# Values stationary, normed probabilities moving in the attention, and other positions of the mixer's stages

## The chip, the core and the metric

The kernel runs on one core of a Trainium2 chip. The metric is the device time of one execution in microseconds. Before the change it is 1552.36 us, the median of three runs (1552.14 to 1554.68).

A core has engines that work side by side, each through its own queue in order: TensorE (PE; its weight loads are PEld), VectorE (DVE), ScalarE (ACT), GpSimd (POOL) and SyncE (SP), which issues nearly all DMAs here. [...] An instruction at the head of a queue that waits holds up everything behind it.

## What is computed

One layer of a decoder: half a SwiGLU step, a mixer with two branches, half a SwiGLU step, norms around them. 512 real positions and 16 meta tokens, width 1024. The change lies in the attention branch of the mixer: 16 query heads of 64, two key/value groups, a window of 128 positions, meta tokens always visible, and a sink per head.

```python
q, kq, vq, rw, gates = jnp.split(u @ w_in[l], cols, axis=-1)
att = sliding_window_attention(rope(q), rope(kq), vq, sinks[l])
rwo = rwkv7_time_mix(*lerped(rw), ...)        # the other branch, a recurrence over time
merged = (jax.nn.sigmoid(g_att) * (att @ w_attn_branch[l])
          + jax.nn.sigmoid(g_rwkv) * (rwo @ w_rwkv_branch[l]))
h = h + merged @ w_out[l]

def sliding_window_attention(q, k, v, sinks):  # per block of queries, per head
    m = jnp.maximum(jnp.max(s, axis=-1, keepdims=True), sink)
    e = jnp.exp(s - m)
    p = e / (jnp.sum(e, axis=-1, keepdims=True) + jnp.exp(sink - m))
    o = jnp.einsum('bnhgqs,bnshd->bnqhgd', p, vals)
```

(The calls are shortened here.) All of it is float32.

## The kernel before

Three stages follow each other: FFN 1 (to about 425 us of the span), the mixer (to about 1130) and FFN 2. The dense products everywhere are made of three passes, L155 to L157: each weight is split into a high part `whi` (L144, ScalarE) and a low part `wlo` (L145, VectorE), each activation into `uh` and `ul`.

The mixer is written as generators: `qkv`, then for each of eight pairs of heads j the stages `stage_a1`, `stage_p`, `stage_i`, `stage_b`, `stage_t` of the recurrent branch, and beside them `att` (the function `attend`, in eight parts), `gate`, `att_branch`, `reload` and `rwkv_branch`. `run` steps through them: always the generator whose next step has the lowest position. `PLAN` gives each an offset and a span in units of one j, `STEPS` the number of steps that share the span, `SHIFT` a correction for one stage of one j, `ATTS` and `GATE` the distance between parts, and `LATE` moves the priority of what a stage issues. The tile scheduler then orders each engine's queue by priority and by what it takes to be ready. So a change of a table moves instructions on all queues.

What the steps of the prediction touch:

- `attend` works on blocks of 64 queries (b = 0 to 7), each in two passes i. A pass handles four of the eight query heads of each key/value group. L567, twice a pass: scores, 128 rows (2 heads x 64 queries) by two groups by n keys, n = 80, 144, then 208. L569: mask and maximum on VectorE. L582: four exponentials on ScalarE, which also give the sums. L584, L585: sink added, reciprocal `rsum`. L591: transposes of the unnormed probabilities, at most 128 keys at a time (one or two parts), L593: copy to `pT`. L600: the value product. L603: normalisation. L608: two transposes. L611: copy. L613: two stores to `aD` in HBM. All PSUM tiles of `attend` come from one bank (`att`), so each must be read before the next is written.
- `stage_b` is the recurrence of pair j over nine chunks: L928 (TensorE), L929 copy of z (ScalarE), L936 (TensorE), L937 and L938 copies into W (VectorE, ScalarE), L941 (TensorE), L947 (L945 in the first chunk) the next W (VectorE). Each step needs the one before.
- `stage_i` inverts triangular blocks on VectorE: L865 loads `LT` from HBM, then L870 and L872 alternate 31 times. `LT` has one buffer, which the end of the stage before (L898, L908) still reads.
- `att_branch` reads `aD` in eight pieces and multiplies by the branch weights `wa`, whose rows `prepare` has put in the order in which `aD` holds the heads.

Of the kernel before, what the change touches and what calls it, by code (L numbers as in the profile page):

```python
# [8 lines left out]
F32 = mybir.dt.float32  # L9
# [4 lines left out]
OP = mybir.AluOpType  # L14
# [3 lines left out]
P = 128  # L18
D = 1024
# [9 lines left out]
CH = 64  # L29
# [7 lines left out]
RB = {"g1": 2, "g2": 2, "W": 2, "g3": 2}  # L37
COUNTS = []
PAUSE = {"sq": 1, "rn": 1, "el": 1, "inv": 1}
PLAN = {"qkv": (-2.771, 0.729), "stage_a1": (-2.83, 0.789), "stage_p": (-1.171, 0.942), "stage_i": (-2.734, 0.587),  # L40
        "stage_b": (-0.138, 0.693), "stage_t": (1.478, 0.214), "att": (-1.614, 1.044), "gate": (0.091, 0.42),
        "att_branch": (3.86, 1.399), "reload": (6.425, 0.417), "rwkv_branch": (7.903, 0.124)}
STEPS = {"qkv": 30, "stage_a1": 19, "stage_p": 13, "stage_i": 9, "stage_b": 27, "stage_t": 5, "att": 13, "gate": 2, "att_branch": 24, "reload": 7,
         "rwkv_branch": 16}

SHIFT = {("stage_t", 5): -0.415, ("stage_i", 7): 0.482, ("stage_b", 2): 0.071, ("stage_a1", 6): -0.027, ("stage_i", 4): -0.133,
        ("stage_t", 2): -0.095, ("stage_b", 3): 0.119, ("stage_p", 1): 0.042, ("stage_t", 4): 0.123, ("stage_t", 3): -0.157,
        ("stage_t", 0): 0.003, ("stage_i", 6): 0.096, ("stage_p", 2): 0.173, ("stage_i", 3): -0.27, ("stage_i", 2): -0.033,
        ("stage_a1", 3): 0.319, ("stage_p", 6): 0.183, ("stage_a1", 4): 0.07, ("stage_p", 3): -0.095, ("stage_i", 1): 0.055,
# [2 lines left out]
        ("stage_t", 7): -0.124, ("stage_t", 1): -0.07, ("stage_i", 0): 0.174, ("stage_p", 5): -0.03, ("stage_b", 7): -0.047}  # L52

FIRST = [(0, 0), (0, 1), (1, 0), (1, 1), (27, 0)]
ATTS = 0.946
GATE = 0.462
LATE = {"gate": 337, "att_branch": 1714, "reload": 1055, "rwkv_branch": 2849, "stage_a1": -79, "stage_t": 196, "stage_p": -207,
        "stage_i": -1108, "qkv": -36, "att": 209, "stage_b": 148}
S_DECAY = float(np.exp(np.float32(-0.5)))
GN_EPS = 64e-5  # L60
RMS_EPS = 1e-6
# [47 lines left out]
def hybrid_layer(ctx: ExitStack, tc: tile.TileContext, a, phases="all"):  # L109
    nc = tc.nc  # L110
    g = Ctx()
# [9 lines left out]
    bank = lambda: sm.tile([P, 512], F32, name="pn")  # L121
# [219 lines left out]
    aD = a["aD"] if "aD" in a else dram.tile([P, KD, SEQ], F32, name="aD")  # L341
# [4 lines left out]
    ident = C("ident")  # L346

    LO, HI = slice(0, 64), slice(64, 128)
# [4 lines left out]
    def mixer(nm):  # L353
# [7 lines left out]
        ap = es.enter_context(tc.tile_pool(name="mx_a", bufs=2))  # L361
# [3 lines left out]
        def bank(tag):  # L365
            if tag in SMALL:
                return small[:, SMALL[tag]]
            return ps.tile([P, 512], F32, name="p" + tag, tag=tag, bufs=BANKS[tag])
# [168 lines left out]
        def attend():  # L537
# [3 lines left out]
            for b in range(NCH):  # L541
# [18 lines left out]
                for i in range(2):  # L560

                    st = ap.tile([P, 2, 2, 208], F32, name="st", bufs=1)
                    mx = ap.tile([P, 2, 2], F32, name="mx")
                    for k in range(2):
                        pt = bank("att")[:, :416].rearrange("p (g s) -> p g s", g=2)
                        hp = 2 * i + k
                        nc.tensor.matmul(pt[:, :, :n], qb[:, P * hp:P * hp + P], kx[:, :, :n], start=True, stop=True)  # L567
                        for kv in range(2):
                            nc.vector.tensor_tensor_reduce(out=st[:, kv, k, :n], in0=pt[:, kv, :n], in1=am, scale=0.125,  # L569
                                                           scalar=NEG, op0=OP.add, op1=OP.max, accum_out=mx[:, kv, k:k + 1])  # L570
                        yield
                    sink = vec[:, VEC["sink"]:VEC["sink"] + 8].rearrange("p (g i k) -> p i g k", g=2, i=2)[:, i]
                    nm = ap.tile([P, 2, 2], F32, name="nm")
                    sm = ap.tile([P, 2, 2], F32, name="sm")
                    rsum = ap.tile([P, 2, 2], F32, name="rsum")
                    nc.vector.tensor_max(out=mx, in0=mx, in1=sink)
                    nc.vector.tensor_scalar(out=nm, in0=mx, scalar1=-1.0, scalar2=None, op0=OP.mult)
                    nc.vector.tensor_sub(out=sm, in0=sink, in1=mx)
                    nc.scalar.activation(out=sm, in_=sm, func=AF.Exp)
                    for x in range(4):  # L580
                        kv, k = x // 2, x % 2
                        nc.scalar.activation(out=st[:, kv, k, :n], in_=st[:, kv, k, :n], func=AF.Exp, bias=nm[:, kv, k:k + 1],  # L582
                                             accum_out=rsum[:, kv, k:k + 1])
                    nc.vector.tensor_add(out=rsum, in0=rsum, in1=sm)  # L584
                    nc.vector.reciprocal(out=rsum, in_=rsum)  # L585
                    yield
                    pTs = []
                    for q, (k0, k1) in enumerate(parts):
                        pt = bank("att")
                        for x in range(4):  # L590
                            nc.tensor.transpose(out=pt[:k1 - k0, P * x:P * x + P], in_=st[:, x // 2, x % 2, k0:k1], identity=ident)  # L591
                        pT = ap.tile([P, 512], F32, name="pT")
                        nc.scalar.copy(out=pT[:k1 - k0], in_=pt[:k1 - k0])  # L593
                        pTs.append(pT)
                    yield
                    po = bank("att")[:, :4 * CH].rearrange("t (p d) -> t p d", p=4)
                    for x in range(4):
                        kv = x // 2
                        for q, (k0, k1) in enumerate(parts):
                            nc.tensor.matmul(po[:, x, :], pTs[q][:k1 - k0, P * x:P * x + P], vt[:k1 - k0, q, CH * kv:CH * kv + CH],  # L600
                                             start=(q == 0), stop=(q == len(parts) - 1))
                    on = ap.tile([P, 4, CH], F32, name="ao", bufs=1)
                    nc.vector.tensor_tensor(out=on, in0=po, in1=rsum.rearrange("p g k -> p (g k)").unsqueeze(2).to_broadcast([P, 4, CH]),  # L603
                                            op=OP.mult)
                    yield
                    pt = bank("att")
                    for kv in range(2):
                        nc.tensor.transpose(out=pt[:, P * kv:P * kv + P], in_=on[:, 2 * kv:2 * kv + 2, :].rearrange("t p d -> t (p d)"),  # L608
                                            identity=ident)
                    ao = ap.tile([P, 2, 2, CH], F32, name="ao", bufs=1)  # L610
                    nc.scalar.copy(out=ao, in_=pt[:, :4 * CH].rearrange("p (g x t) -> p g x t", g=2, t=CH))  # L611
                    for kv in range(2):
                        nc.sync.dma_start(out=aD[:, 4 * kv + 2 * i:4 * kv + 2 * i + 2, CH * b:CH * b + CH], in_=ao[:, kv])  # L613
                    yield

        def gates():
# [444 lines left out]
        for j in range(NJ):  # L1061
            if j:
                ts.append(g[0])
            g = ()
# [110 lines left out]
def prepare(x, meta_tokens, norm_ffn1, ffn1_w_in, ffn1_w_out, norm_mix, w_in, rwkv_mu, sinks, w0, w2, a0, a2, g2, k_k, k_a,  # L1175
# [29 lines left out]
    b = np.concatenate([g2[0][P:]] * 3 + [np.zeros((32, D), np.float32)], 0)  # L1205
    d["g2s"] = np.ascontiguousarray(np.stack([g2[0][:P], b], 1).reshape(P, 2, KD, P).transpose(2, 0, 1, 3))

    wa = w_attn_branch.reshape(1, 4, 2, 2, CH, D).transpose(0, 1, 3, 2, 4, 5).reshape(1, D, D)
    for n, w in (("wa", wa), ("wr", w_rwkv_branch), ("wo", w_out)):
        d[n] = pack_w(w[0])  # L1210
    return d
# [17 lines left out]
```

## Time and profile before

| what | value |
|---|---|
| median of three runs | 1552.36 us |
| the profiled execution's own time | 1557.82 us |
| its span, first to last instruction | 1556.1 us |
| mean granted clock of TensorE | 0.980 |
| instructions | 25641 |
| HBM read, written | 140.03 MB, 21.52 MB |

The profile is one execution, 5.4 us over the median; a sum made from its rows is made against 1557.82. In a row of a group stand the source line, the engine and operation, the tile written and the tiles read (their numbers left out), the size, the count, then times. "PE patt L600: 8.5, 6" under such rows means: 8.5 us of idle time, in 6 places, ended when that instruction was done. In the timeline the last bracket is the idle time of the engine before the row and what ended it; "x16" joins 16 like instructions that follow each other. A matmul's own duration overlaps with its neighbours', so the distance from one start to the next is what counts. f32 matmuls appear in the trace as two passes, transposes as one.

### The profile page before, as it was taken

The numbers are of one execution on the slowest core, as the hardware profiler recorded it, in microseconds if no ns is written. First come the engines' busy times: TensorE is split into PE (matmuls) and PEld (weight loads), VectorE is DVE, ScalarE is ACT, GpSimd is POOL, SyncE is SP. The second block draws the span as 40 slices with busy tenths as digits, with TensorE's granted clock in tenths as the row PEclk, the third lists the DMA queues.
The fourth block names the chain that finished last, engine by engine and source line by source line (L and its number), as shares of the span: only waits on it lengthen the run. The fifth ranks groups of instructions, "written<-read, shape, count | busy, mean of one in ns | idle before, by whom it ended". The sixth has DMA issues, their size and how long they took to land. (4 is left out here: it accounts for less than half of the span.)

```text
span 1556.1 us, 25641 instructions
## 1 busy us (share of the span) xinstructions
PE 1500.3 (96%) x9365; PEld 1325.2 (85%) x9365; DVE 900.1 (58%) x2471; ACT 652.9 (42%) x1468; POOL 93.6 (6%) x153
## 2 busy tenths in 40 slices
PE   9999999999999999998999999999999999999997
PEld 9999999999887888887878887677777888888886
DVE  6334334344764886887978888675655444443334
ACT  5333333233442457465664754635343333332231
POOL 0111111000100000000000000000000111110000
PEclk9999999999999999999989999999999999999998
DMA  5333333344243333323332232555633333333332
GB/s 165 89 93 91 89 93 88 110 120 116 78 121 96 112 84 89 81 81 104 99 98 76 82 101 85 153 183 173 221 95 89 95 95 96 97 97 91 95 97 79
DMA packets 137838, 163.23 MB, mean 105 GB/s; under 512 B 56960, under 2 KB 68288, under 8 KB 137712
## 3 DMA queue, kind: packets, MB, share of 16 engines
q1 hardware_dynamic: 137568, 161.54, 35.4%
q8 instruction: 73, 1.20, 0.3%
q14 instruction: 53, 0.43, 0.1%
q10 hardware_dynamic: 144, 0.06, 0.0%
HBM read 140.03 MB, written 21.52 MB: 104 GB/s over the span
## 5 line engine op out<-in xcount | busy, mean ns | idle before, releaser
L144 ACT CAST whi<-raw 128x512 fp32r<-128x512 f32 (+1 forms) x426 | 258.8, 611 | 576.6 <-PE dn L156 446.5
L145 DVE TENSOR_TENSOR wlo<-raw,whi 128x512 fp32r<-128x512 f32 (+1 forms) x426 | 287.9, 679 | 304.1 <-ACT whi L144 300.0
L155 PE MATMUL dn<-uh,whi 128*128 128x264 f32 (+1 forms) x1320 | 426.8, 323 | 1.9 <-DVE tgt L657 0.9
L156 PE MATMUL dn<-ul,whi 128*128 128x264 f32 (+1 forms) x1320 | 427.3, 324 | 0.3 <-DVE ul L203 0.3
L157 PE MATMUL dn<-uh,wlo 128*128 128x264 f32 (+1 forms) x1320 | 425.0, 322 | 0.0
L155 PEld LDWEIGHTS dn<-uh,whi 128*128 128x128 f32 x1320 | 247.8, 188 | 23.9 <-ACT whi L144 3.2
L157 PEld LDWEIGHTS dn<-uh,wlo 128*128 128x128 f32 x1320 | 248.4, 188 | 19.9
L156 PEld LDWEIGHTS dn<-ul,whi 128*128 128x128 f32 x1320 | 248.4, 188 | 19.0 <-DVE ul L203 0.5
L155 PE MATMUL pdn<-uh,whi 128*128 128x264 f32 (+3 forms) x656 | 229.0, 350 | 4.6 <-ACT whi L144 2.5
L157 PE MATMUL pdn<-uh,wlo 128*128 128x264 f32 (+3 forms) x656 | 224.3, 343 | 3.7 <-DVE wlo L145 3.6
L156 PE MATMUL pdn<-ul,whi 128*128 128x264 f32 (+3 forms) x656 | 224.5, 343 | 0.9 <-DVE ul L253 0.8
L155 PEld LDWEIGHTS pdn<-uh,whi 128*128 128x128 f32 x656 | 127.1, 194 | 17.0 <-ACT whi L144 4.2
L157 PEld LDWEIGHTS pdn<-uh,wlo 128*128 128x128 f32 x656 | 127.0, 194 | 11.4 <-DVE wlo L145 5.0
L156 PEld LDWEIGHTS pdn<-ul,whi 128*128 128x128 f32 x656 | 126.7, 193 | 7.7 <-DVE ul L253 1.7
L155 PE MATMUL dn<-mh,whi 128*128 128x264 f32 (+2 forms) x350 | 110.7, 316 | 0.0
L156 PE MATMUL dn<-ml,whi 128*128 128x264 f32 (+2 forms) x350 | 110.6, 316 | 0.0
L157 PE MATMUL dn<-mh,wlo 128*128 128x264 f32 (+2 forms) x350 | 110.5, 316 | 0.0
L285 POOL TENSOR_TENSOR sg<-sg,rstd 128x528 f32<-128x528 f32 (+1 forms) x44 | 58.0, 1319 | 595.8 <-ACT sg L284 428.9
L286 DVE TENSOR_TENSOR m<-sg,dn 128x528 f32<-128x528 f32 (+1 forms) x44 | 30.6, 696 | 70.9 <-PE dn L157 67.6
L155 PEld LDWEIGHTS dn<-mh,whi 128*128 128x128 f32 x350 | 66.1, 189 | 4.4
L156 PEld LDWEIGHTS dn<-ml,whi 128*128 128x128 f32 x350 | 66.1, 189 | 4.3
L157 PEld LDWEIGHTS dn<-mh,wlo 128*128 128x128 f32 x350 | 66.0, 189 | 4.3
(395 smaller groups left out, 2058.2 us busy)
## 6 DMA issues: line engine op xcount, KB each, us to landing
raw<-win SPq DMA_DIRECT2D x104, 256.0 KB
raw<-w1in SPq DMA_DIRECT2D x88, 256.0 KB
raw<-w2in SPq DMA_DIRECT2D x88, 256.0 KB
raw<-w1out SPq DMA_DIRECT2D x40, 256.0 KB
raw<-w2out SPq DMA_DIRECT2D x40, 256.0 KB
gD<-tgt SPq DMA_DIRECT2D x24, 256.0 KB
raw<-wa SPq DMA_DIRECT2D x16, 256.0 KB
tgt<-gD SPq DMA_DIRECT2D x16, 256.0 KB
```

The lines of the kernel that those rows point to most:

```text
L144: nc.scalar.copy(out=hi, in_=raw)
L145: (eng or nc.vector).tensor_tensor(out=lo, in0=raw, in1=hi.bitcast(F32), op=OP.subtract)
L155: nc.tensor.matmul(o, hi, xh[k][:, c], start=(k == 0), stop=False)
L156: nc.tensor.matmul(o, hi, xl[k][:, c], start=False, stop=False)
L157: nc.tensor.matmul(o, lo, xh[k][:, c], start=False, stop=last)
L285: nc.gpsimd.tensor_mul(out=sg, in0=sg, in1=nm.rstd[:, :n])
L286: nc.vector.tensor_mul(out=vw(m), in0=vw(sg), in1=vu)
```

## The change

The probabilities are normed before they are transposed: VectorE multiplies all 4n scores of a pass by `rsum` instead of the 256 outputs. The value product has its operands exchanged: the values of both groups (`vt`, keys by 128) are the stationary operand, the transposed probabilities (keys by 512) move. The output then has the head dimension on the partitions: group 0 in the lower 64, group 1 in the upper, and both groups are computed for all four quarters of columns, of which half is used. The two transposes back (L608) are gone; two copies of 64 x 256 pick the used halves; one store replaces two. `prepare` orders the rows of the branch weights to fit. Five entries of `PLAN` and more get other positions, and four of `LATE` change by over 100.

```diff
-PLAN = {"qkv": (-2.771, 0.729), "stage_a1": (-2.83, 0.789), "stage_p": (-1.171, 0.942), "stage_i": (-2.734, 0.587),
+PLAN = {"qkv": (-2.771, 0.729), "stage_a1": (-2.739, 0.789), "stage_p": (-1.216, 0.942), "stage_i": (-2.722, 0.829),
...
-LATE = {"gate": 337, "att_branch": 1714, "reload": 1055, "rwkv_branch": 2849, "stage_a1": -79, "stage_t": 196, "stage_p": -207,
-        "stage_i": -1108, "qkv": -36, "att": 209, "stage_b": 148}
+LATE = {"gate": 160, "att_branch": 1506, "reload": 494, "rwkv_branch": 3893, "stage_a1": -79, "stage_t": 196, "stage_p": -207,
+        "stage_i": -958, "qkv": -42, "att": 209, "stage_b": 148}
...
                     nc.vector.reciprocal(out=rsum, in_=rsum)
+                    sv = st.rearrange("p g k s -> p (g k) s")[:, :, :n]
+                    nc.vector.tensor_tensor(out=sv, in0=sv, in1=rsum.rearrange("p g k -> p (g k)").unsqueeze(2).to_broadcast([P, 4, n]),
+                                            op=OP.mult)
                     yield
...
-                    po = bank("att")[:, :4 * CH].rearrange("t (p d) -> t p d", p=4)
-                    for x in range(4):
-                        kv = x // 2
-                        for q, (k0, k1) in enumerate(parts):
-                            nc.tensor.matmul(po[:, x, :], pTs[q][:k1 - k0, P * x:P * x + P], vt[:k1 - k0, q, CH * kv:CH * kv + CH],
-                                             start=(q == 0), stop=(q == len(parts) - 1))
-                    on = ap.tile([P, 4, CH], F32, name="ao", bufs=1)
-                    nc.vector.tensor_tensor(out=on, in0=po, in1=rsum.rearrange("p g k -> p (g k)").unsqueeze(2).to_broadcast([P, 4, CH]),
-                                            op=OP.mult)
+                    po = bank("att")
+                    for q, (k0, k1) in enumerate(parts):
+                        nc.tensor.matmul(po, vt[:k1 - k0, q, :], pTs[q][:k1 - k0], start=(q == 0), stop=(q == len(parts) - 1))
                     yield
-                    pt = bank("att")
-                    for kv in range(2):
-                        nc.tensor.transpose(out=pt[:, P * kv:P * kv + P], in_=on[:, 2 * kv:2 * kv + 2, :].rearrange("t p d -> t (p d)"),
-                                            identity=ident)
-                    ao = ap.tile([P, 2, 2, CH], F32, name="ao", bufs=1)
-                    nc.scalar.copy(out=ao, in_=pt[:, :4 * CH].rearrange("p (g x t) -> p g x t", g=2, t=CH))
-                    for kv in range(2):
-                        nc.sync.dma_start(out=aD[:, 4 * kv + 2 * i:4 * kv + 2 * i + 2, CH * b:CH * b + CH], in_=ao[:, kv])
+                    ao = ap.tile([P, 4, CH], F32, name="ao", bufs=1)
+                    pv = po.rearrange("p (g x t) -> p g x t", g=2, t=CH)
+                    for kv, rows in enumerate((LO, HI)):
+                        nc.scalar.copy(out=ao[rows], in_=pv[rows, kv])
+                    nc.sync.dma_start(out=aD[:, 4 * i:4 * i + 4, CH * b:CH * b + CH], in_=ao)
...
-    wa = w_attn_branch.reshape(1, 4, 2, 2, CH, D).transpose(0, 1, 3, 2, 4, 5).reshape(1, D, D)
+    wa = w_attn_branch.reshape(1, 2, 8, CH, D).transpose(0, 2, 1, 3, 4).reshape(1, D, D)
```

In the changed kernel all lines behind the edit have numbers lower by five (L870 is L865, L937 is L932, L947 is L942), the multiply is L587, the transposes of the probabilities are L594, the value product is L602.

TensorE's queue before, around the value product of block 3, second pass (`patt` is its PSUM tile, `pn` and `py` those of stage_b, `pdn` a dense tile):

```order
L936 MATMUL pn<-zy,xt_4608 128x128
L600 MATMUL patt<-vt,pT 128x64 x5
L941 MATMUL py<-W,g_7360 128x64 x2
L600 MATMUL patt<-vt,pT 128x64 x2
L155 MATMUL pdn<-uh,whi 128x264
```

and behind 25 more rows:

```order
L600 MATMUL patt<-vt,pT 128x64
L156 MATMUL pdn<-ul,whi 128x512
L157 MATMUL pdn<-uh,wlo 128x512
L936 MATMUL pn<-zy,xt_4608 128x128
L608 MATMUL patt<-con,ao 128x128 x2
```

The same pass in the changed kernel:

```order
L157 MATMUL pdn<-uh,wlo 128x512
L155 MATMUL pdn<-uh,whi 128x512
L602 MATMUL patt<-pT,vt 128x512
L931 MATMUL pn<-zy,xt_4608 128x128
L602 MATMUL patt<-pT,vt 128x512
L936 MATMUL py<-W,g_7248 128x64 x2
L708 MATMUL pdn<-xa,wa2h 128x264
```

Eight value matmuls of 64 columns have become two of 512, and the transposes L608 behind the next step of the recurrence are gone.

VectorE's queue before, at the start of stage_i of pair 3 (L870 reads `LT` when its load has landed; L603 is the normalisation of the pass above; L937 is the recurrence's write to W):

```order
L969 TENSOR_TENSOR tys<-tys,gy 128x512
L870 TENSOR_TENSOR xtmp<-LT,X 102x31
L872 TENSOR_TENSOR X<-X,xtmp 102x31
L870 TENSOR_TENSOR xtmp<-LT,X 102x30
L603 TENSOR_TENSOR ao<-patt,rsum 128x256
L872 TENSOR_TENSOR X<-X,xtmp 102x30
L446 SCALAR_TENSOR_TENSOR tk<-pdn,omm,tm 128x264
L870 TENSOR_TENSOR xtmp<-LT,X 102x29
L937 COPY W<-pn 64x64
```

The same place in the changed kernel:

```order
L446 SCALAR_TENSOR_TENSOR tk<-pdn,omm,tm 128x264
L932 COPY W<-pn 64x64
L587 TENSOR_TENSOR st<-st,rsum 128x832
L942 SCALAR_TENSOR_TENSOR W<-py,f,sf 64x64 x2
L964 TENSOR_TENSOR tys<-tys,gy 128x512
L145 TENSOR_TENSOR wlo<-raw,whi 128x512
L865 TENSOR_TENSOR xtmp<-LT,X 102x31
L932 COPY W<-pn 64x64
L867 TENSOR_TENSOR X<-X,xtmp 102x31
```

The normalisation stands ahead of stage_i's start, on the 832 scores, with two W writes right behind it, and a W write is the first row behind the one that waits for `LT`.

VectorE's queue before, at the start of stage_i of pair 4:

```order
L446 SCALAR_TENSOR_TENSOR tk<-pdn,omm,tm 128x264
L335 SCALAR_TENSOR_TENSOR gy<-gt,gy 128x8
L937 COPY W<-pn 64x64
L870 TENSOR_TENSOR xtmp<-LT,X 102x31
L584 TENSOR_TENSOR rsum<-rsum,sm 128x4
L792 SCALAR_TENSOR_TENSOR kbt<-tal,tE_9024 64x8x64
L872 TENSOR_TENSOR X<-X,xtmp 102x31
```

and in the changed kernel:

```order
L336 TENSOR_SCALAR gy<-gy 128x8
L964 TENSOR_TENSOR tys<-tys,gy 128x512
L865 TENSOR_TENSOR xtmp<-LT,X 102x31
L940 TENSOR_SCALAR W<-py,f 64x64
L867 TENSOR_TENSOR X<-X,xtmp 102x31
L940 TENSOR_SCALAR W<-py,f 64x64
L865 TENSOR_TENSOR xtmp<-LT,X 102x30
```

The start of stage_i 4 has moved ahead, from between two chunks of the recurrence of pair 3 to its first chunk, whose two W writes (L940) now stand behind it.

More of the change, by code (lines that the diff above doesn't have):

```diff
@@ L39 @@
 PAUSE = {"sq": 1, "rn": 1, "el": 1, "inv": 1}
-PLAN = {"qkv": (-2.771, 0.729), "stage_a1": (-2.83, 0.789), "stage_p": (-1.171, 0.942), "stage_i": (-2.734, 0.587),
-        "stage_b": (-0.138, 0.693), "stage_t": (1.478, 0.214), "att": (-1.614, 1.044), "gate": (0.091, 0.42),
-        "att_branch": (3.86, 1.399), "reload": (6.425, 0.417), "rwkv_branch": (7.903, 0.124)}
+PLAN = {"qkv": (-2.771, 0.729), "stage_a1": (-2.739, 0.789), "stage_p": (-1.216, 0.942), "stage_i": (-2.722, 0.829),
+        "stage_b": (-0.138, 0.693), "stage_t": (1.506, 0.214), "att": (-1.58, 1.044), "gate": (0.038, 0.42),
+        "att_branch": (3.892, 1.15), "reload": (6.343, 0.409), "rwkv_branch": (7.953, 0.128)}
 STEPS = {"qkv": 30, "stage_a1": 19, "stage_p": 13, "stage_i": 9, "stage_b": 27, "stage_t": 5, "att": 13, "gate": 2, "att_branch": 24, "reload": 7,
          "rwkv_branch": 16}
-SHIFT = {("stage_t", 5): -0.415, ("stage_i", 7): 0.482, ("stage_b", 2): 0.071, ("stage_a1", 6): -0.027, ("stage_i", 4): -0.133,
+SHIFT = {("stage_t", 5): -0.415, ("stage_i", 7): 0.482, ("stage_b", 2): 0.071, ("stage_a1", 6): -0.027, ("stage_i", 4): -0.297,
         ("stage_t", 2): -0.095, ("stage_b", 3): 0.119, ("stage_p", 1): 0.042, ("stage_t", 4): 0.123, ("stage_t", 3): -0.157,
@@ L54 @@
 FIRST = [(0, 0), (0, 1), (1, 0), (1, 1), (27, 0)]
-ATTS = 0.946
+ATTS = 0.961
 GATE = 0.462
-LATE = {"gate": 337, "att_branch": 1714, "reload": 1055, "rwkv_branch": 2849, "stage_a1": -79, "stage_t": 196, "stage_p": -207,
-        "stage_i": -1108, "qkv": -36, "att": 209, "stage_b": 148}
+LATE = {"gate": 160, "att_branch": 1506, "reload": 494, "rwkv_branch": 3893, "stage_a1": -79, "stage_t": 196, "stage_p": -207,
+        "stage_i": -958, "qkv": -42, "att": 209, "stage_b": 148}
 S_DECAY = float(np.exp(np.float32(-0.5)))
```

## The prediction

> **What bounds the kernel now.** First the head of the page, then the windows of the mixer, the only stage that the change touches.
>
> ```profile
> span 1556.1 us, 25641 instructions
> PE 1500.3 (96%) x9365; PEld 1325.2 (85%) x9365; DVE 900.1 (58%) x2471; ACT 652.9 (42%) x1468; POOL 93.6 (6%) x153
> PE   9999999999999999998999999999999999999997
> ```
>
> TensorE is busy for 96% of the span, and no slice of the forty falls under 80%. What TensorE has to do is therefore the first term. The second is what it loses in the mixer, which the windows show (span; busy us of PE, PEld, DVE, ACT, POOL; granted clock; DMA share and rate):
>
> ```profile
> 440.00:560.00 120.00, 112.50 (x676) 99.18 (x675) 82.31 (x225) 47.94 (x108) 5.82 (x20) 0.94 0.36 102
> 560.00:700.00 140.00, 135.34 (x924) 118.13 (x923) 111.43 (x442) 82.86 (x246) 8.19 (x23) 0.99 0.31 88
> 700.00:850.00 150.00, 140.09 (x939) 121.58 (x938) 122.62 (x465) 83.32 (x239) 8.17 (x25) 0.97 0.34 94
> 850.00:1000.00 150.00, 140.92 (x875) 117.81 (x873) 116.81 (x457) 87.38 (x262) 6.70 (x15) 0.95 0.34 96
> 1000.00:1140.00 140.00, 132.36 (x609) 104.73 (x610) 91.66 (x245) 62.03 (x140) 0.74 (x1) 0.96 0.58 186
> ```
>
> In these 700 us PE is idle for 700 - 661.2 = 38.8 us, and the clock that is not granted is worth 120 x 0.06 + 140 x 0.01 + 150 x 0.03 + 150 x 0.05 + 140 x 0.04 = 26.2 us. So the mixer pays 65 us for waits, 0.68 us of clock with each idle us. VectorE (524.8 us busy) has 175 us of air there and ScalarE (363.5) 336 us. Neither is a bound by its sum; both can be late at one instruction. Where they are late, the waits say:
>
> ```profile
> PEld pn L936 <- ACT zy L929: 10.0, 30, 1.0
> PEld py L941 <- DVE W L937: 9.8, 16, 2.7
> PEld pn L928 <- DVE W L947: 7.6, 10, 3.0
> DVE xtmp L870 <- DMA LT<-Ls: 10.8, 5, 2.8
> DVE xtmp L870 <- issue: 3.2, 1, 3.2
> DVE xtmp L870 <- DMA vt<-vD: 2.7, 1, 2.7
> ```
>
> The first three are the recurrence of stage_b: TensorE, ScalarE, TensorE, VectorE, in turn. The last three are one thing: the first L870 of a stage_i stands at the head of VectorE's queue until the load of LT lands, 16.7 us in seven stops. Everything behind it waits too, the recurrence's writes to W among it:
>
> ```profile
> 796.83 0.19 DVE L870 TENSOR_TENSOR xtmp<-LT,X 102x31 f32<-102x31 f32 x1 [3.17 <-issue]
> 799.00 0.65 PE L928 MATMUL pn<-W,g1e 128*128 128x64 f32 x2 [2.74 <-DVE W L947]
> 796.30:799.00 2.70, 0.01 (x1) 0.01 (x1) 2.17 (x11) 0.73 (x2) 0.00 (x0) 1.00 0.14 52
> 799.00:809.30 10.30, 10.30 (x43) 9.71 (x44) 5.52 (x22) 4.82 (x13) 0.00 (x0) 0.50 0.19 61
> ```
>
> Such a hole costs PE 2.7 us and then half the clock for a while: here 10.3 us at 0.50, worth 5.2. At the stage's mean of 0.68 us a hole costs 2.7 x 1.68 = 4.5 us; I use that below.
>
> **The change, part by part.** *TensorE.* The trace shows the 120 value matmuls as 240 passes, two to an f32 matmul. These rows give what a pass and a transpose take, from one start to the next:
>
> ```profile
> L600 PE MATMUL patt<-vt,pT x240: 217/275/421, 553.3 to 982.1; 80*128 80x64 f32 x56, 128*128 128x64 f32 x56, 16*128 16x64 f32 x8
> 980.34 2.00 PE L600 MATMUL patt<-vt,pT 128*128 128x64 f32 x16
> 982.14 0.48 PE L155 MATMUL pdn<-uh,whi 128*128 128x512 f32 x1
> 565.39 0.38 PE L608 MATMUL patt<-con,ao 128*128 128x128 f32 x2
> 565.61 0.39 PE L817 MATMUL ps<-g1o,kbt 128*128 128x128 f32 x2
> 648.57 1.02 PE L828 MATMUL ps<-tsx,con 128*128 128x512 f32 x2
> 649.42 0.27 PE L837 MATMUL ps<-con,kbt 128*128 128x128 f32 x1
> ```
>
> Sixteen 64-column passes take 982.14 - 980.34 = 1.80 us, 0.1125 each; two transposes 0.22 us. Removed: 240 x 0.1125 + 32 x 0.11 = 30.5 us. Added: 30 matmuls whose moving tile is the probabilities, 512 wide. L828 is an f32 matmul of that shape: two passes in 649.42 - 648.57 = 0.85 us. 30 x 0.85 = 25.5 us. The columns double, and still the sum falls by 5.0 us, because a 64-column pass takes as long as a 128-column one. Eight of the removed matmuls have only 16 rows; if their 16 passes cost nothing, the gain is 3.2. Ends 3.2 and 5.0; 224 of 240 passes are like the row, so I take **-4.5 us**.
>
> The Trainium skill, page "TensorE: Matmul & The Clock Gate", section "Back-to-back issue gap", speaks against this change: it prices a lone warm matmul by its columns, with about 60 cycles for 64 of them and 518 for 512. By an estimate from it, the 240 passes cost 240 x 25 ns = 6 us, the new 60 cost 60 x 216 ns = 13 us, and the sum would gain where I let it fall. Its section "LDWEIGHTS (loading the stationary operand)" sets a load at columns / 1.2 ns, 107 ns for 128; the 0.1125 of the row agrees with that one.
>
> *VectorE, ScalarE, SyncE.*
>
> ```profile
> L603 DVE TENSOR_TENSOR ao<-patt,rsum x16: 374/424/425, 554.4 to 983.0; 128x256 f32<-128x256 f32 x16
> L751 DVE TENSOR_TENSOR tE<-tE,cm x8: 682/692/701, 448.1 to 887.2; 128x520 f32<-128x520 f32 x8
> L611 ACT COPY ao<-patt x16: 358/372/374, 556.0 to 983.9; 128x256 f32<-128x256 f32 x16
> L853 ACT COPY W<-ps x16: 349/368/369, 538.4 to 980.7; 64x256 f32<-64x256 f32 x16
> L613 SPq DMA_DIRECT2D aD<-ao x32: 370/424/2062, 556.4 to 984.7; - x32
>   PE patt L600: 8.5, 6
> ```
>
> The multiply by 1/sum moves from 256 output elements to 4n scores: 320 and 576 (twice each), 832 (12 times). Between L603 (256: 0.424) and L751 (520, also with a broadcast factor: 0.692) an element takes 1.015 ns, so 832 take 1.01 us, 576 0.75, 320 0.49: 14.6 us against 16 x 0.424 = 6.8. VectorE gets **+7.8 us** of work. It loses a wait at the same time: L603 held the queue's head 8.5 us for the value matmuls (last row), and the new multiply reads only what the exponentials left. ScalarE gets two copies of 64x256 for one of 128x256: 16 x 0.37 = +5.9 us. SyncE issues 16 stores fewer, 16 x 0.42 = 6.8 us. I cost all this at **0 on the path**: the air above (175 and 336 us) covers it. Where the cover is missing, a multiply directly ahead of a W write that TensorE waits for costs 1.01 - 0.42 = 0.6 us; if none of the 16 were covered, 14.6 us; if the freed 8.5 us all reached TensorE, -8.5.
>
> *The added wait.* The transposes of the probabilities (L591, now L594) used to wait for the exponentials and now wait for the multiply too: 1.01 us, plus the sum and the reciprocal ahead of it. Behind them on TensorE stands everything, in order. The scheduler has moved them back: between a pass's last score matmul and its first transpose the order has 14 to 72 TensorE rows before (median 34.5) and 31 to 148 now (52.5). Eighteen rows, at 140.09 us / 939 = 0.15 us of the third window, are 2.7 us, more than the wait adds. Cost 0; the present wait there is small:
>
> ```profile
>   ACT st L582: 3.8, 7
> ```
>
> If none of it were covered, 16 x 1.3 = 21 us, which the row makes unlikely.
>
> *The wait of the dropped transposes.*
>
> ```profile
> PE patt L608 <- DVE ao L603: 2.6, 1, 2.6
> 735.35 0.44 PE L608 MATMUL patt<-con,ao 128*128 128x128 f32 x2 [2.58 <-DVE ao L603]
> 735.81 0.21 DVE L937 COPY W<-pn 64x64 f32<-64x64 f32 x1
> 736.32 0.33 PE L941 MATMUL py<-W,g 128*128 128x64 f32 x2
> ```
>
> With L608 gone, three dense matmuls (0.77 us) would run early; then L941 needs the W copy, which stands in the same queue behind the same L870 and ends at 736.02. Late next is W, 0.3 us earlier than now. Bounds 0 and 2.6; I take **-0.3 us**. In the new order this place has W (L932) as the very next row behind the wait.
>
> *The moved positions.* No stage gets an instruction more. The loads of LT, the recurrence and the dense tiles are the same, and what sits between them is shuffled. Counted in the order of VectorE: a W write is the row directly behind the LT wait in 1 of 8 stages before, in 4 of 8 now. That is no price, since W was also late from further back (799.00 above). I take **0**, with two holes either way, 2 x 4.5 = 9.0 us, as both ends.
>
> Sum: 1557.8 (the profiled execution: span 1556.1 and 1.7 around it) - 4.5 - 0.3 = 1553.0. The profiled execution is 5.4 us over the median of the three runs, 1552.4, so the forecast is **1547.6 us**.
>
> **Rivals.**
> - *The recurrence sets the mixer, not TensorE's sum.* Then the 4.8 us go into waits of L936, L941 and L928. For it: 27 us of waits in their three rows, and VectorE at 122.6 of 150 us in the third window. Against: between them PE runs dense matmuls back to back, which do get shorter in sum. Time 1552.4.
> - *Slower: two LT holes more reach TensorE.* Place: W writes behind the first L865 (L870 before) of stages j = 2, 3, 4 and 7. Price 2 x 4.5 = 9.0, so 1556.6; it decides from 4.8 / 4.5 = 1.1 holes on. For it: the count 4 against 1, and the longer multiply directly ahead of W writes in three of 16 passes. Against: holes reach PE already in most stages.
> - *Faster: two holes fewer*, since VectorE's head no longer waits for the value matmuls. 1547.6 - 9.0 = 1538.6.
> - *A pass costs by its columns.* At L828's 0.85 / 2 / 512 = 0.83 ns a column, the 240 passes were 240 x 64 x 0.83 ns = 12.7 us; then PE gets 25.5 - 12.7 - 3.5 = +9.3, and 1552.4 + 9.3 = 1561.7. The 0.1125 us speak against it.
>
> On the clock, the same page of the Trainium skill, section "What's actually happening", has the clock halved after at least one idle window of about 3.4 us. Here 2.70 us of idle time were enough for 10.3 us at 0.50; the trace decides. By the page, holes under 3.4 us might cost no clock, and the slower rival would be 5.4 us instead of 9.0.
>
> **How the numbers follow.** Forecast 0.42; recurrence 0.22; two holes more 0.15; two fewer 0.19; columns 0.02. About 0.2% (3.1 us) is what a measurement of this kernel tells from no change: under 1549.3 is faster, over 1555.5 slower. Nine tenths of the forecast's share and all of the faster rival make 0.57 faster; the rest of the forecast and the recurrence 0.26 the same; 0.17 slower. Range 1539 to 1557: it takes in the slower rival and nearly the faster one.
>
> **What will show it.** The value matmuls: 60 passes near 0.43 us apart, no L608. VectorE: 16 multiplies, up to 1.01 us, sum 14.6. The first L865 of a stage still idles VectorE by 2.5 to 3.2 us. The mixer's PE idle time near 39 us and its clock loss near 26; if these move by over 9 us together, the positions decided and my zero for them is the wrong step. If 64-column passes turn out to have been hidden, the first term is.

## The result and the profile after

The changed kernel takes 1564.09 us (median of four runs, 1562.02 to 1566.86), beside 1553.52 for the kernel before on the same chip (four runs, 1552.14 to 1555.03). The ratio is 1.0058, 95% interval 1.0037 to 1.0079. It is slower by some 9 us where I forecast 5 us faster; the range ended at 1557.

The profiled execution of the changed kernel (1562.02) is the fastest of its four; that of before (1557.82) was the slowest of its runs. So the two profiles show 4.2 us of a difference that is about 9. The head of the page, and the same five windows of the mixer as before (span; busy us of PE, PEld, DVE, ACT, POOL; granted clock; DMA share and rate):

```profile
span 1560.3 us, 25194 instructions
PE 1492.9 (96%) x9153; PEld 1298.2 (83%) x9153; DVE 909.8 (58%) x2471; ACT 660.3 (42%) x1484; POOL 93.0 (6%) x153
PE   9999999999998999998999999999999999999997
```

```profile
440.00:560.00 120.00, 107.82 (x645) 94.48 (x644) 79.80 (x217) 46.14 (x102) 5.76 (x20) 0.94 0.36 100
560.00:700.00 140.00, 131.96 (x838) 109.00 (x837) 112.19 (x437) 85.41 (x255) 7.36 (x21) 0.99 0.33 92
700.00:850.00 150.00, 138.78 (x870) 114.14 (x869) 123.02 (x470) 86.44 (x244) 8.73 (x26) 0.97 0.31 88
850.00:1000.00 150.00, 140.24 (x829) 110.91 (x827) 126.35 (x462) 89.85 (x264) 7.11 (x17) 0.99 0.34 97
1000.00:1140.00 140.00, 131.23 (x608) 103.09 (x608) 90.53 (x250) 60.30 (x142) 0.74 (x1) 0.96 0.59 185
```

PE is busy 7.4 us less (1500.3 before), VectorE 9.7 more (900.1), ScalarE 7.4 more (652.9). In the 700 us PE idles for 700 - 650.0 = 50.0 us, 11.2 more than before. The clock not granted is worth 120 x 0.06 + 140 x 0.01 + 150 x 0.03 + 150 x 0.01 + 140 x 0.04 = 20.2 us, 6.0 less. So the waits grew, and the clock hid half of that in this one execution.

Where TensorE waits, on its own row of the groups (columns: count, busy us, mean ns, idle time just before them and what ended it). First the kernel before, then the changed one:

```profile
L155 PE MATMUL pdn<-uh,whi 128*128 128x264 f32 (+3 forms) x656 | 229.0, 350 | 4.6 <-ACT whi L144 2.5 <-DVE h L294 0.8 <-DVE tE L496 0.7
L591 PE MATMUL patt<-con,st 128*80 128x128 f32 (+2 forms) x120 | 24.9, 284 | 1.2 <-ACT st L582 1.2
L608 PE MATMUL patt<-con,ao 128*128 128x128 f32 x32 | 7.2, 306 | 2.9 <-DVE ao L603 2.6 <-DVE nt L334 0.2
```

```profile
L155 PE MATMUL pdn<-uh,whi 128*128 128x264 f32 (+3 forms) x656 | 226.9, 349 | 15.7 <-ACT whi L144 8.7 <-DVE tk L446 2.2 <-ACT tE L513 1.4
L594 PE MATMUL patt<-con,st 128*80 128x128 f32 (+2 forms) x120 | 22.3, 287 | 1.7 <-DVE st L587 1.3 <-ACT pT L596 0.2 <-ACT tm L445 0.2
```

Ahead of the first dense pass stand 11.1 us more (4.6 to 15.7), of them 6.2 in waits for the high part of a weight (2.5 to 8.7). More than half of the 11.1 is one hole. The timeline around it, on SyncE (SPq), ScalarE and TensorE, and the clock behind it:

```profile
471.37 0.47 SPq L533 DMA_DIRECT2D qD<-tys  x1
471.88 1.05 SPq L533 DMA_DIRECT2D qD<-pT  x1
473.03 1.36 SPq L143 DMA_DIRECT2D raw<-win  x3
...
476.76 1.26 ACT L144 CAST whi<-raw 128x512 fp32r<-128x512 f32 x2 [4.57 <-DMA raw<-win]
...
477.43 0.80 PE L155 MATMUL pdn<-uh,whi 128*128 128x512 f32 x1 [5.82 <-ACT whi L144]
...
475.40:482.20 6.80, 4.77 (x11) 3.77 (x12) 1.34 (x2) 1.24 (x2) 0.00 (x0) 0.50 0.49 166
```

Three weight loads are issued at 473.03, behind eight stores to qD that themselves waited for VectorE. The weights land at 476.8, ScalarE splits them, and TensorE has stood for 5.82 us; then it runs at half clock to 482.2. Before the change those three loads stood ahead of these stores in SyncE's order, and there was no such hole.

The weight loads' own waits, for the recurrence, and VectorE's waits at the first L865 of `stage_i`:

```profile
PEld pn L931 <- ACT zy L924: 15.8, 43, 1.2
PEld py L936 <- DVE W L932: 14.3, 30, 2.2
PEld pdn L155 <- ACT whi L144: 10.4, 4, 6.0
PEld pn L923 <- DVE W L942: 5.0, 11, 1.5
DVE xtmp L865 <- DMA LT<-Ls: 10.5, 6, 3.0
DVE xtmp L865 <- DMA raw<-win: 3.5, 1, 3.5
DVE xtmp L865 <- issue: 2.2, 1, 2.2
```

VectorE waits for LT as before: 16.2 us (10.5 + 3.5 + 2.2) against 16.7. The recurrence's weight loads wait for zy and W more often (43 and 30 times against 30 and 16). Most of that is covered by the matmul ahead, which still runs: on PE's own rows the idle time ahead of the recurrence's matmuls is 14.9 us now and was 18.0 (the sum over the groups of its three lines).

The parts that were priced:

```profile
L602 PE MATMUL patt<-pT,vt 80*128 80x512 f32 (+2 forms) x60 | 31.7, 626 | 1.3 <-ACT pT L596 1.3
L587 DVE TENSOR_TENSOR st<-st,rsum 128x832 f32<-128x832 f32 (+2 forms) x16 | 14.6, 913 | 0.1
L607 ACT COPY ao<-patt 64x256 f32<-64x256 f32 x32 | 11.7, 367 | 14.5 <-PE patt L602 14.3
815.80 1.08 PE L602 MATMUL patt<-pT,vt 128*128 128x512 f32 x2
816.72 0.33 PE L923 MATMUL pn<-W,g1e 128*128 128x64 f32 x2
740.20 0.43 PE L936 MATMUL py<-W,g 128*128 128x64 f32 x2 [1.83 <-DVE W L932]
```

There are 60 passes and no L608. The multiplies sum to 14.6 us, as priced; the copies to 11.7 us (16 x 0.37 twice). A value matmul of full height takes 816.72 - 815.80 = 0.92 us to the next start.

### The profile page after: what moved, and what is told of

It reads as the page before. It is cut to its first block, busy times and chain, and to the rows that moved or that the text cites. A ratio compares the mean times of both kernels' runs of the same rounds, so it can differ in the third digit from the quotient of the medians.

```text
span 1560.3 us, 25194 instructions
## 1 busy us (share of the span) xinstructions
PE 1492.9 (96%) x9153; PEld 1298.2 (83%) x9153; DVE 909.8 (58%) x2471; ACT 660.3 (42%) x1484; POOL 93.0 (6%) x153
## 5 line engine op out<-in xcount | busy, mean ns | idle before, releaser
L155 PE MATMUL dn<-uh,whi 128*128 128x264 f32 (+1 forms) x1320 | 426.8, 323 | 1.9 <-DVE h L1127 0.9
L155 PEld LDWEIGHTS dn<-uh,whi 128*128 128x128 f32 x1320 | 247.8, 188 | 24.0 <-ACT whi L144 3.2
L155 PE MATMUL pdn<-uh,whi 128*128 128x264 f32 (+3 forms) x656 | 226.9, 349 | 15.7 <-ACT whi L144 8.7
L156 PE MATMUL pdn<-ul,whi 128*128 128x264 f32 (+3 forms) x656 | 220.2, 338 | 1.1 <-DVE ul L253 1.1
L155 PEld LDWEIGHTS pdn<-uh,whi 128*128 128x128 f32 x656 | 125.2, 192 | 29.2 <-ACT whi L144 10.4
L155 PE MATMUL dn<-mh,whi 128*128 128x264 f32 (+2 forms) x350 | 110.7, 316 | 0.0
L155 PEld LDWEIGHTS dn<-mh,whi 128*128 128x128 f32 x350 | 66.1, 189 | 4.3
```

Source lines behind the costliest of these rows:

```text
L155: nc.tensor.matmul(o, hi, xh[k][:, c], start=(k == 0), stop=False)
L156: nc.tensor.matmul(o, hi, xl[k][:, c], start=False, stop=False)
```

## The experiments

Each version's profiled execution gives four numbers that answer to each other: the span, PE's busy time, the idle time (the difference) and the work (busy time less span x (1 - mean granted clock), good to about 0.8 us, since the clock is given to 0.001). "Old code" is the attention before, "new code" the changed one; a version that only moves a number of the tables does the same work in another order. Each row's last three columns are of one execution; the old code's work, the same by its instructions, still spreads from 1467.6 to 1475.3 in them, so single rows say little and means more.

| version | code | what is moved | ratio, 95% interval | span | idle | work |
|---|---|---|---|---|---|---|
| before | old | | 1 | 1556.1 | 55.8 | 1469.2 |
| e10 | old | stage_t 191 | 0.9998, 0.9984 to 1.0013 | 1556.5 | 60.1 | 1473.1 |
| e9 | old | GATE 0.466 | 1.0020, 1.0010 to 1.0029 | 1557.9 | 56.3 | 1472.0 |
| e6 | old | ATTS 0.950 | 1.0021, 1.0004 to 1.0037 | 1560.3 | 56.9 | 1470.6 |
| e5 | old | att 204 | 1.0090, 1.0055 to 1.0125 | 1566.8 | 60.2 | 1475.3 |
| e14 | old | stage_a1 -2.739 | 1.0123, 1.0100 to 1.0146 | 1576.1 | 63.5 | 1471.6 |
| e2 | old | all the new tables | 1.0131, 1.0094 to 1.0167 | 1579.8 | 69.5 | 1467.6 |
| after | new | all the new tables | 1.0058, 1.0037 to 1.0079 | 1560.3 | 67.4 | 1469.5 |
| e1 | new | none, the old tables | 1.0044, 1.0029 to 1.0059 | 1566.3 | 68.4 | 1465.0 |
| e13 | new | new tables, stage_a1 -2.83 | 1.0053, 1.0035 to 1.0070 | 1562.5 | 65.5 | 1465.8 |
| e8 | new | new tables, ATTS 0.957 | 1.0063, 1.0044 to 1.0082 | 1565.6 | 71.5 | 1465.9 |
| e12 | new | new tables, stage_t 191 | 1.0076, 1.0050 to 1.0102 | 1566.7 | 73.2 | 1466.9 |
| e7 | new | new tables, att 204 | 1.0084, 1.0056 to 1.0112 | 1564.7 | 73.3 | 1467.9 |
| e11 | new | new tables, GATE 0.466 | 1.0109, 1.0080 to 1.0138 | 1577.4 | 71.8 | 1463.0 |

**The change in its halves: e1 and e2.** e1 is the new code under the old tables, e2 the old code under the new ones. The tables' part of the change is larger than told above: nine of the eleven entries of `PLAN`, one of `SHIFT`, `ATTS`, and six of `LATE`, five of them by over 100.

> The new attention code with the positions (PLAN, SHIFT, ATTS, LATE) of before. If the positions cost the time: about 1549 us, TensorE's smaller sum shows (-4 against before). If the code costs it (the longer multiply and the 512-column products hold VectorE's and ScalarE's queues ahead of the recurrence): 1562 to 1566, as the whole change. If any reordering loses, because the old tables fitted the old code: between, 1555 to 1562.

> The old attention code with the positions of after. If the positions cost the time: 1565 or more (+12 to +15), with the hole of about 5.8 us before the weights near 477 us in it. If the code costs it: 1553, as before. If any reordering loses: 1555 to 1562.

e1 runs at 1.0044, e2 at 1.0131. The halves don't add up: the code alone costs 0.44%, the tables alone 1.31%, both together 0.58%. Under the old tables the new code is 0.44% slower than the old; under the new tables it is 0.7% faster (1.0058 against 1.0131, intervals apart). Put the other way, the new tables cost the new code 0.14%, with intervals that overlap. So the loss is there without any moved table, and the sign of what the code is worth hangs on the tables.

**The multiply: e3, e4, e16.** e3 puts the multiply into the old code and lets VectorE only copy the outputs. e4 is the changed kernel without the multiply; e16 the same under the old tables (so beside e1).

e3 as lines on the kernel before:

```diff
+sv = st.rearrange("p g k s -> p (g k) s")[:, :, :n]
+nc.vector.tensor_tensor(out=sv, in0=sv, in1=rsum.rearrange("p g k -> p (g k)").unsqueeze(2).to_broadcast([P, 4, n]), op=OP.mult)
...
-nc.vector.tensor_tensor(out=on, in0=po, in1=rsum.rearrange("p g k -> p (g k)").unsqueeze(2).to_broadcast([P, 4, CH]), op=OP.mult)
+nc.vector.tensor_copy(out=on, in_=po)
```

> Before, with the probabilities normed ahead of their transposes (the 4n-element multiply) and the 256 outputs copied by VectorE instead of multiplied; value products, transposes back and tables as before. VectorE gets 14.6 us more. If the longer multiply ahead of W writes is the cost: +6 to +10 us. If VectorE's air covers it: within 2 us of before.

> The changed kernel with the multiply left out: the probabilities stay unnormed, so the attention output lacks its division by the sum. VectorE gets 14.6 us less than in the changed kernel. If the multiply is the cost: 1554 or less (-10 against the changed kernel). If the positions are: 1560 to 1564, almost as the changed kernel.

> The new code under the old tables without the multiply: the division by the sum is left out, so the output lacks it. Against e1, which has it (1.0044). Theory A: no hole near 477 us, no multiply: 1.000 to 1.003. Theory B, the multiply costs most of it: 0.996 to 0.999, under before by TensorE's gain. If it stays at 1.004 or above, neither is the cause and other waits of the order are.

e3: 1.0096 (1.0075 to 1.0118), some 15 us, more than either of my cases. e4: 1.0014 (0.9999 to 1.0029), so 0.44% or 7 us under the changed kernel, clear of noise and between my two cases. e16: 1.0031 (1.0013 to 1.0048), only 0.13% under e1, with intervals that overlap. The multiply's price depends on the order it is taken from, and since leaving it out also lays the queues anew, its own part in the 7 us is not shown. The idle time stays at 66.7 (e4) and 67.1 (e16), that of the new code with the multiply.

**A hair's breadth: e5 to e12.** Each moves one number a little, the same number in the old code and in the new (`ATTS` up by 0.004 in the old, down by 0.004 in the new). e5, and e7 likewise in the changed kernel's line:

```diff
-        "stage_i": -1108, "qkv": -36, "att": 209, "stage_b": 148}
+        "stage_i": -1108, "qkv": -36, "att": 204, "stage_b": 148}
```

> Before with one number moved by a hair: LATE of att 204 for 209. The work is the same to the instruction; the queues' orders differ in thousands of rows. If the order as such is worth microseconds, and that of before is a lucky or fitted one: +4 to +15 us. If only the positions of the change are costly: within 2 us of before.

> Before with ATTS 0.95 for 0.946, a second hair. Same expectations: +4 to +15 us if before stands on a fitted order, within 2 us if not.

> The changed kernel with LATE of att 204 for 209. If after has no fitted order, a hair moves it either way, by 2 to 8 us. If its positions are the costly thing: within 2 us of the changed kernel. If after too is fitted: slower by 4 or more.

> The changed kernel with ATTS 0.957 for 0.961. Same expectations as for the run before it.

> The kernel before, with GATE 0.466 for 0.462: the same work on every engine in another order. Theory, order as such decides and the kernel before stands on an order that suits it: 2 to 15 us over before, with PE busy unchanged and the mixer's idle time and clock loss together 2 to 15 us over its 67. Rival, the new code itself costs the time: within 2 us of before, and the two moved versions of the new code run 8 us or more over the two moved versions of the old.

> The kernel before, with stage_t's LATE 191 for 196, a smaller shuffle than the last. Theory: 1 to 15 us over before. Rival, the new code itself costs the time: within 2 us of before.

> The changed kernel, with GATE 0.466 for 0.462. Theory: its order has nothing to lose, so it lands on either side of the changed kernel, between 1555 and 1572 us; over all moved versions, the new code's mean is 2 to 6 us under the old code's, the gain of TensorE's work. Rival: the new code's mean is above the old code's by 5 us or more, since the wait for the multiply goes with every order.

> The changed kernel, with stage_t's LATE 191 for 196. Theory: between 1555 and 1572 us, as for the other moved version of the new code. Rival: over the moved versions of the old code by 8 us or more.

With identical work the old code moves between 0.9998 and 1.0090, the new between 1.0063 and 1.0109. So a hair is worth up to 14 us, more than the change. But my theory of that point fell: I expected the four moved versions of the new code 2 to 6 us under the old code's four. Their mean ratio is 1.0083 against 1.0032 (e5, e6, e9, e10), 0.5% or 8 us over, the size that I had given to the rival, that the new code itself costs. The table's last two columns show both sides of it. Mean work 1465.9 against 1472.7, 6.8 us less: TensorE's gain is there. Mean idle time 72.5 against 58.4, 14.1 us more: it is given back, and more. But four and four are few: the two ranges of ratios overlap, and with e2, e14, e1, e13 and the changed kernel itself the means are 1.0064 (old, six) and 1.0070 (new, seven). So that the new code costs by itself is not shown. All four moved versions of the new code are also slower than the changed kernel, by 0.05 to 0.51%, so its tables may be fitted to it as well; e1 and e13, with older numbers, are not slower.

**The hole near 477 us: e13 and e14.** One number places it: the start of stage_a1 in `PLAN`. e13 takes it back in the changed kernel, e14 brings it to the kernel before. e14's edit:

```diff
-PLAN = {"qkv": (-2.771, 0.729), "stage_a1": (-2.83, 0.789), "stage_p": (-1.171, 0.942), "stage_i": (-2.734, 0.587),
+PLAN = {"qkv": (-2.771, 0.729), "stage_a1": (-2.739, 0.789), "stage_p": (-1.171, 0.942), "stage_i": (-2.734, 0.587),
```

> The changed kernel, with the start of stage_a1 in PLAN back at -2.83 (-2.739 in the change). This puts three weight loads back ahead of the second group of qD stores on SyncE. Theory A, the tables' hole near 477 us costs: the hole goes, and with it 4 to 9 us, to 1555 to 1560 (ratio 0.9995 to 1.0035). Theory B, the multiply's wait and other waits of the new code cost, the hole is made good later: ratio 1.005 to 1.009 as the other versions of the new code.

> The kernel before, with the start of stage_a1 at the change's -2.739 for -2.83: the hole near 477 us is opened in the old code. Theory A: PE idles about 6 us near 477 us, and the kernel runs 4 to 9 us over before (1.003 to 1.006). Theory B: the hole is there, but the ratio stays within 1.002, like three of the other small moves of the old code.

The hole follows the number in both. The dense matmuls' group in e13:

```profile
L155 PE MATMUL pdn<-uh,whi 128*128 128x264 f32 (+3 forms) x656 | 229.6, 352 | 8.5 <-ACT whi L144 3.3 <-ACT uh L252 1.6 <-DVE tk L446 0.9
```

and e14: its head, the rows around its hole, the waits of TensorE's loads and three windows of its mixer:

```profile
span 1576.1 us, 25679 instructions
PE 1512.6 (96%) x9365; PEld 1332.8 (85%) x9365; DVE 902.8 (57%) x2471; ACT 655.1 (42%) x1468; POOL 92.7 (6%) x153
...
472.38 1.37 SPq L143 DMA_DIRECT2D raw<-win  x3
...
476.40 0.79 PE L155 MATMUL pdn<-uh,whi 128*128 128x512 f32 x1 [5.88 <-ACT whi L144]
...
PEld pn L936 <- ACT zy L929: 16.3, 40, 1.4
PEld pn L928 <- DVE W L947: 10.4, 14, 2.6
...
440.00:560.00 120.00, 108.28 (x629) 95.76 (x628) 76.12 (x203) 44.89 (x100) 5.74 (x20) 0.91 0.34 98
560.00:700.00 140.00, 131.53 (x834) 113.80 (x833) 101.97 (x406) 78.18 (x233) 5.39 (x19) 0.93 0.30 84
700.00:850.00 150.00, 137.81 (x878) 117.73 (x878) 118.50 (x461) 81.50 (x233) 8.31 (x23) 0.93 0.29 84
```

Closing the hole in the new code gains nothing that can be measured (1.0053 against 1.0058), although the group's idle time falls from 15.7 to 8.5. Opening it in the old code costs 1.23%, some 19 us, nearly all that the tables as a whole cost there (e2, 1.31%). A hole of 5.88 us can't be 19 us by itself: the clock is at 0.91 to 0.93 through three windows (before 0.94, 0.99, 0.97), and waits for zy and W grow. In e13 the case without a price for the hole came true (1.005 to 1.009); in e14 neither did (up to 1.002, or 1.003 to 1.006). The hole is no fixed price; the number lays the whole mixer anew.

**Where the added work stands: e15, e17, e18.** All have e13's tables. e15 gives the multiply to ScalarE, e18 to GpSimd; e17 gives the two copies of the output to VectorE.

The edits on e13, in the order e15, e17, e18:

```diff
-nc.vector.tensor_tensor(out=sv, in0=sv, in1=rsum.rearrange("p g k -> p (g k)").unsqueeze(2).to_broadcast([P, 4, n]), op=OP.mult)
+for x in range(4):
+    kv, k = x // 2, x % 2
+    nc.scalar.mul(out=st[:, kv, k, :n], in_=st[:, kv, k, :n], mul=rsum[:, kv, k:k + 1])
...
-nc.scalar.copy(out=ao[rows], in_=pv[rows, kv])
+nc.vector.tensor_copy(out=ao[rows], in_=pv[rows, kv])
...
-nc.vector.tensor_tensor(out=sv, in0=sv, in1=rsum.rearrange("p g k -> p (g k)").unsqueeze(2).to_broadcast([P, 4, n]), op=OP.mult)
+nc.gpsimd.tensor_tensor(out=sv, in0=sv, in1=rsum.rearrange("p g k -> p (g k)").unsqueeze(2).to_broadcast([P, 4, n]), op=OP.mult)
```

> As e13, with the multiply of the scores by 1/sum made by ScalarE, four operations a pass, and none of it on VectorE. VectorE's busy time falls by about 15 us, ScalarE's rises by 16 x 4 x 0.3 to 0.5, 19 to 32 us. Theory A: the same as e13 within 3 us. Theory B, if it is VectorE's queue that the multiply holds up: 4 us or more under e13, though the transposes wait longer; if it is the wait of the transposes: 2 us or more over e13.

> As e13 (1.0053), with the two copies of the attention's output made by VectorE instead of ScalarE: VectorE takes the wait for the value matmuls, as L603 had it in the kernel before. Theory S, ScalarE's stops hold up zy and the weights behind them: 3 to 7 us under e13 (ratio 1.001 to 1.0035), with TensorE's waits for zy falling from e13's size by 3 us or more. Theory O, the order in which the work happens to fall decides: anywhere between 1.000 and 1.011, without that fall.

> As e13 (1.0053), with the multiply of the scores made by GpSimd, which is busy for under 2% of the mixer: 14.7 us leave VectorE, and the transposes wait longer by GpSimd's slower operation. Theory V, the multiply in VectorE's queue costs: 3 us or more under e13. Theory T, the transposes' wait costs: 3 us or more over e13, and the waits of L594 grow by as much. Theory O: between 1.000 and 1.011, with neither.

e15: 1.0045 (1.0026 to 1.0063). e17: 1.0082 (1.0052 to 1.0111). e18: 1.0050 (1.0034 to 1.0066). The groups of the multiply and the transposes in e18, with one multiply and VectorE's row beside it, and the multiply in e15:

```profile
L587 POOL TENSOR_TENSOR st<-st,rsum 128x832 f32<-128x832 f32 (+2 forms) x16 | 24.2, 1510 | 107.9 <-DVE rsum L585 61.9 <-DVE xtmp L865 13.8 <-ACT zy L924 8.2
L594 PE MATMUL patt<-con,st 128*80 128x128 f32 (+2 forms) x120 | 21.3, 283 | 5.2 <-POOL st L587 5.1
...
745.57 1.57 POOL L587 TENSOR_TENSOR st<-st,rsum 128x832 f32<-128x832 f32 x1 [8.32 <-DVE xtmp L865]
745.34 0.21 DVE L865 TENSOR_TENSOR xtmp<-LT,X 102x54 f32<-102x54 f32 x1
745.59 1.62 DVE L867 TENSOR_TENSOR X<-X,xtmp 102x54 f32<-102x54 f32 x1
```

```profile
L588 ACT ACTIVATE st<-st,rsum 128x208 f32<-128x208 f32 (+2 forms) x64 | 24.1, 438 | 4.0 <-DVE rsum L585 3.8
```

Beside e13's 1.0053, neither placing of the multiply gains or loses anything measurable. On GpSimd the transposes wait 5.1 us for it, and the total is the same. But e18 doesn't relieve VectorE: its busy time is 910.8 us against 909.1 in e13, though 14.7 us of multiplies are gone. While GpSimd multiplies, a step of the inversion on VectorE lasts until GpSimd is done, 1.62 us for 0.21 in the rows above, and the two steps (L865, L867) sum to 116.5 us where e13 has 107.8. So e18 can't tell what VectorE's queue costs. (GpSimd is busy for 29.6 of the mixer's 700 us in the kernel before, 4%, not under 2%.) That leaves e15 for this question, and there ScalarE is busy for 22.3 us more (683.5 against 661.2). The copies on VectorE (e17) are no better, and the waits of TensorE's loads for zy don't fall (17.4 us, 16.1 in e13). TensorE's idle time is 65.5 (e13), 69.1 (e15), 67.4 (e17), 70.4 (e18): it doesn't leave with any of the pieces. No version of the new code that does all of the work is as fast as the kernel before; only e4, whose output lacks the division, can't be told from it.

## Why the prediction was wrong

**The step that failed** is "*The moved positions.* ... I take **0**, with two holes either way, 2 x 4.5 = 9.0 us, as both ends". I took the mixer's waits and clock as a constant of the kernel, and the order as noise about it. It isn't the moved tables alone: the new code under the old ones (e1) already loses 0.44%. What I had at 0 is the price of a new order, whether the tables or the code make it. The runs show:

- The waits moved by more than TensorE's work. In the pair of profiles idle time went from 55.8 to 67.4 us. Over the seven versions of the new code with unchanged work (after, e1, e7, e8, e11, e12, e13) it is 65.5 to 73.3, over the six moved versions of the old code 56.3 to 69.5. The means are 70.2 and 61.1, 9.1 us apart.
- The ends were too narrow. One number of the change, alone in the old code, costs 1.23%, some 19 us (e14), twice my end of 9.0.
- The kernel before is not a neutral point. Five of the six moved versions of the old code are slower, and one is the same. Their mean is 1.0064 with e2 and e14, which carry the change's own numbers, and 1.0032 without. So on these six a mere reordering loses 0.3 to 0.6% on average: 5 to 10 us, as much as the gain that I had counted or more.

**My own test of this step was blunt.** I had written that it fell if idle time and clock loss moved by over 9 us together. In the windows they moved by +11.2 - 6.0 = 5.2, since one grew and the other shrank in that execution.

**TensorE's term** was right in its mechanism and about right in size. I had 25.5 us for the 30 value matmuls; the distances from start to next start sum to 27.6, 0.92 a matmul where I had 0.85. In the old code the 240 passes sum to 30.0 in the same way, and the 32 transposes were 3.5. That is a fall of 30.0 + 3.5 - 27.6 = 5.9 beside my 4.5, with stretches of half clock in both. The table's work agrees: its mean falls by 5.4 (1471.7 over the six old, 1466.3 over the seven new). The pair alone would not have shown it (1469.2 to 1469.5): the changed kernel has the highest work of the new code, and before has less than all of the old code but e2. The rival that prices passes by columns is refuted: it put the 240 passes at 12.7 us and forecast 9.3 us more work.

**VectorE, ScalarE and SyncE at 0** is neither shown nor refuted. The multiply sums to 14.6 us as priced. Moved to ScalarE it costs the same (e15 against e13); left out, it brings nothing measurable under the old tables (e16 against e1), but 7 us under the change's own (e4), which is within my bound of 14.6 and may be the order again. What is not zero is the wait of the transposes, which I had also put at 0: 1.2 to 1.7 us in the pair, but 4.7 on average over the seven new versions and 1.9 over the six old ones (the idle time of L594 and L591).

**The dropped wait** went as told, but not its price. At the same place W is late next, and TensorE waits 1.83 us at 740.20 where it waited 2.58 for L603. That is 0.75 gained at the spot, for the 0.3 that I took. The clock behind it took that back: full after the old hole, half for 3.4 us after the new one, worth 1.7. First before, then the changed kernel:

```profile
735.30:742.00 6.70, 6.65 (x39) 5.25 (x39) 6.34 (x29) 6.35 (x17) 0.10 (x1) 1.00 0.51 153
741.60:745.00 3.40, 3.40 (x10) 2.52 (x11) 2.48 (x11) 2.70 (x7) 0.00 (x0) 0.50 0.31 113
```

So my 4.5 us a hole, waits and clock together, is a mean that single holes don't keep to.

**The rivals.** The LT holes did not multiply: 16.2 us on VectorE against 16.7, and PE's idle time ahead of the recurrence's matmuls fell (18.0 to 14.9). So the slower case that I had priced is not the one that came. Closest is the first rival, that waits eat the gain: over the families, idle time +9.1 stands against -5.4 of work and -3.6 of clock (33.4 to 29.8), and the mean spans are equal, 1566.2 and 1566.2. But it had the place wrong. It put the waits at the recurrence's matmuls, and there PE idles 16.4 us on average in the old versions and 16.8 in the new. The growth is spread: +4.0 ahead of the first dense passes (L155), +2.8 ahead of the transposes, +1.7 and +1.2 ahead of other stages' matmuls (`ps` and `pt`).

**What stays open** is why the new code has more idle time on average, with the multiply (65.5 to 73.3) and without it (66.7 and 67.1). Of the old code only e2 (69.5) reaches that range, and under those same tables the new code idles less (67.4). That the 240 short value passes used to fill gaps between dependent steps, and 60 dense ones don't, would fit; I have no run that shows it. Nor can the 0.58% be split cleanly: by the ratios it is the distance of before from the mean of its moved versions, plus the distance of the two families, less what the changed kernel lies under the mean of its own. With the four and four that were moved by a hair this is 0.32 + 0.51 - 0.25; with all six and seven (means 1.0064 and 1.0070) it is 0.64 + 0.06 - 0.12.

**One reading** was off, without bearing on the sum: the last of the forty slices of PE's row is at 7, under 80%.

## What to carry to other kernels

Where a kernel's order hangs on a table of numbers, its measured time holds a share that no row of the profile shows: move a table number by a hair in the kernel before, two or three times, before you price an edit. That spread, here 0 to 0.9% for four hairs and 1.2% for one larger step, is the width that a forecast needs. The kernel before stood at its good end; if its tables were fitted, which nothing here shows, that would be the reason, and the first effect of an edit is then a loss. Compare the edited code with the shuffled old code as well as with the tuned one: the first tells whether the idea saves work, the second only whether it does so under these tables.

## What the runs showed of the hardware

- A short idle stretch can be followed by half the clock, and need not be. In the changed kernel TensorE idled for 1.81 us up to 946.27 and then ran at half clock; it idled for 2.22 us up to 876.49 and kept the full one. What decides between them is not shown:

```profile
946.27 0.58 PE L936 MATMUL py<-W,g 128*128 128x64 f32 x2 [1.81 <-DVE W L932]
946.40:949.80 3.40, 3.40 (x14) 2.99 (x15) 3.22 (x12) 2.36 (x6) 0.00 (x0) 0.50 0.05 16
876.49 0.39 PE L155 MATMUL pdn<-uh,whi 128*128 128x264 f32 x1 [2.22 <-DVE tk L446]
876.50:880.00 3.50, 3.50 (x29) 3.50 (x30) 3.47 (x15) 1.22 (x3) 0.00 (x0) 1.00 0.03 11
```

In both kernels' mixers every stretch at 0.50 lasts 3.4, 6.8 or 10.2 us. The Trainium skill, page "TensorE: Matmul & The Clock Gate", section "What's actually happening", has a free-running window of 3413 ns, which these lengths agree with. That a whole idle window comes ahead of the throttle is not what these rows show: up to 944.46 TensorE was at work.
- The same 16 multiplies by a broadcast factor, most of 128 x 832, have a mean of 919 ns on VectorE (e13) and 1510 ns on GpSimd (e18); as four operations on ScalarE it is 4 x 438 = 1752 ns (e15).
- GpSimd's multiply holds up VectorE: in e18 an operation of VectorE on 102 x 54 that began 0.02 us behind it took 1.62 us and ended with it, where the one before took 0.21.
- On ScalarE, reading half of the partitions of PSUM (the memory that TensorE's products go to) costs as much as reading all: the copy of 64 x 256 takes 367 ns, that of 128 x 256 took 372.
